# GLA heads in a lane of their own, a later first level, wider steps between mLSTM heads, and an urgent GpSimd multiplication

## The chip, the cores and the metric

One core of one Trainium2 chip runs the whole kernel; the other cores are idle. The metric is the device time of one launch in microseconds. Lower is better.

## What is computed

One inference step of a two-layer trunk, on 512 prompt tokens and 8 sequences of 4 sample tokens, 544 columns in all, in float32 throughout. The first layer's mixer is the place of the change:

```
mq, mk, mv, mo, mi, mf, gq, gk, gv, gg, ga = split(x @ w_in)        # 1024 -> 3096 columns
mLSTM, 4 heads, keys of 64, values of 128:   gates from mi, mf; scores (q k) * exp(decay);
    h = headnorm(num / max(|den|, exp(-m))) * sigmoid(mo)
GLA, 4 heads, keys of 64, values of 128:     la = log_sigmoid(ga @ wa2 + ba) / 16, cumulated to A
    s[t, s'] = sum_k q[t,k] k[s',k] exp(A[t,k] - A[s',k])  for s' <= t
    o = headnorm(s @ v + (q exp(A)) @ S0) * silu(gg)
both also return their last states, for the prompt and for every sample sequence
mix = concat(mLSTM, GLA) @ w_out;  x <- LN(1.414 x + mix);  then a squared-ReLU MLP
```

The second layer is a Mamba-2 mixer with an MLP of its own. The change leaves both, and the first MLP, as they are.

## The kernel before

**The dense work.** Activations lie with features on partitions and tokens in the free dimension, in two halves of 272 columns. A float32 product is made from three products of split operands (`whi`, `wlo` for a weight block, `xh`, `xl` for the activations). So one 128-column block of `w_in` is 2 halves x 8 k-tiles x 3 = 48 matmuls, all on line 378 in `dense`. The first stage, `ab`, has 24 such blocks in the order gq0 gk0 gq1 gk1, gv 0-3, mq, mk, mv 0-3, gg 0-3, mo 0-3. Before each matmul of line 378 stands one `tick()`.

**The lanes.** All other TensorE work of the stage is fed in between by generators. Each lane is a queue of generators; a generator emits some instructions, then yields a number n, and comes on again n + 1 ticks later. `need(keys)` yields 0 until the keys are set. TensorE executes in exactly the order in which this emits (its order is fixed by hand). The order on the other engines, VectorE, ScalarE, GpSimd and the DMA queues, is made by a planner ahead of time: it walks its own estimate of the execution and gives each engine the ready instruction of the highest priority, which is the order of emission, unless a block is marked `high_priority`. At run time every engine then takes its instructions strictly in that order. So an instruction whose input comes later than the planner thought holds all that stand behind it.

**The GLA lane.** `gla_decay` makes A for two feature groups q = 0, 1 (two heads each). `gla_scores` makes for each q the diagonal (`gd`, L1072, multiplied by the identity on L1074 into `sT`) and then nine levels L = 1, 2, 4 ... 256: GpSimd subtracts (`F`, L1083), ScalarE takes two exponentials (L1085, L1086), VectorE makes `zq` (L1090) and `zk` (L1092), TensorE multiplies them (`gs`, L1100 or L1113), and VectorE or ScalarE puts the result into `sT` (L1104, L1107 to L1114). `zq` and `zk` have two buffers each. A level comes 16 ticks after the one before. A transposition (`kdt`, L1122) ends each q. After both q, four heads follow. `head_out` of one head has two parts. The first multiplies the scores with the values (`num`, L868, two PSUM banks), and the headnorm is made from it: VectorE statistics (L872, L873), two ScalarE functions, and `hn` (L896), marked urgent. The second part transposes `hn` (`hot`, L902) and makes `cg` (L904). `pipeline` sets the second part of one head directly in front of the first part of the next, `W["out"]` = 38 apart. Then come the final state (`fst`), the GLA sample tokens and the mLSTM sample tokens, each with six state updates: GpSimd masks the values (`vm`, L1002), TensorE multiplies (`supd`, L1006), and VectorE adds into the state `c` (L1010), which goes out on SyncE's queue (`s_S` or `s_C`, L1015). The state of the mLSTM samples comes in on ScalarE's queue (L962) into the two buffers that held the GLA state.

**The mLSTM lane.** `ml_gates` has four parts of small ScalarE and VectorE work on four partitions (L1220 to L1275); part i waits until the first part of GLA head i has been emitted. The heads wait for the key `"gla"`, set when the last GLA head is done. Each has a broadcast (`rowbc`), scores (`md`, `mo`, L1318 to L1326) and the two parts of `head_out`; `pipeline` staggers them `W["mr"]` = 46 apart.

**Shared buffers.** `F`, `kd`, `hn`, `kz` and `vm` share four buffers (tag `sc`). Small PSUM tiles have four banks, every fifth of them another one.

**The start.** `warm` emits ten matmuls on constants; then the gate projections of the first half (`gate_sums(0)`, L842) come in two parts, 6 and 11 ticks later.

Of the kernel before, what the change touches and what calls it, by code (L numbers as in the profile page):

```python
# [13 lines left out]
ALU = mybir.AluOpType  # L14
# [3 lines left out]
P = 128  # L18
# [14 lines left out]
HEADM = 6  # L33
HEADA = 2

W = dict(dec=12, gates=30, gr=8, sc=16, lev=15, v=24, kd=10, out=38, ss=40, end=12, c0=20, u=13, s=16, ml=12, mr=46, dt=238, sg=72, sx=14, sq=26, so=48, l0=12, l1=12, v0=74, v1=55, f0=16, f1=18, f2=4, ls=20, vs=47)
GATES = ((0, 0, 4), (32, 4, 4), (64, 8, 16))
LEVELS = (64, 32, 16, 8, 4, 2, 1)

# [189 lines left out]
def trunk_kernel(ctx, tc, a, stages=("ab", "mlp0", "ssd", "mlp1")):  # L229
    nc = tc.nc  # L230
    V, S, G, TE = nc.vector, nc.scalar, nc.gpsimd, nc.tensor
# [99 lines left out]
    ready = set()  # L331

    def need(*keys):
        while not ready.issuperset(keys):
            yield 0

    def launch(gen, lane="norm"):
        lanes.setdefault(lane, []).append([next(gen), gen])
# [377 lines left out]
    def ab(pool, early, then):  # L716
# [120 lines left out]
        def gate_sums(hf):  # L837

            ps = pm("gsum")
            for k in range(KT):  # L840
                g = k % 4
                TE.matmul(ps[32 * g:32 * g + 32, :TH], gw[:, k], xs_in[4 * hf + k // 2][:, k % 2], start=k < 4, stop=k >= 4)  # L842
                if k == 3 and hf == 0:
                    yield 11
            with tc.high_priority():
                S.copy(gsum[hf], ps[:, :TH])

# [89 lines left out]
        def sample(key, q_, ksT, kstk, w, wl0, em):  # L937

            st_in, st_out = a["C0" if key == "m" else "S0"], a["s_C" if key == "m" else "s_S"]
            vs = vraw[key]
            nv = 129 if key == "m" else 128
            pbd = small("pbd", [P, NB, 4, LS])
            with hold():
                V.tensor_tensor(pbd, ksT.rearrange("p (b t) -> p b t", t=LS)[:, :, None, :].broadcast_to([P, NB, 4, LS]),
                                hmask[:, None, :, None].broadcast_to([P, NB, 4, LS]), ALU.mult)  # L950
                for q in range(2):
                    qw = small("qw", [P, NS])
                    V.tensor_tensor(qw, q_[q][:, NP:], w[:, q], ALU.mult)
                    for e in range(2):
                        o = 8 * q + 4 * e
                        V.tensor_tensor(Zq[:, q].rearrange("p (r x) -> p r x", r=2)[:, :, :128].rearrange("p r (k c) -> p r k c", k=4)[:, :, :, o:o + LS],
                                        qw.rearrange("p (k r t) -> p r k t", k=4, r=2),
                                        hm[:, e:e + 1, None, None].broadcast_to([P, 2, 4, LS]), ALU.mult)
            c0 = []
            for q in range(2):  # L960
                t = pool.tile([P, NB, 130], F32, tag="z4", name="c0", bufs=2)
                S.dma_start(out=t[:, :, :128], in_=st_in[:, q])  # L962
                if key == "m":
                    V.tensor_copy(t[:, :, 128:129], n0[:, q, :, None])
                c0.append(t)
            yield W["c0"]
            num = pm("snum")
            TE.matmul(num[:, :nv], pbd.rearrange("p b h t -> p (b h t)"), vs[:, :nv], start=True, stop=False)
            for r in range(2):
                for q in range(2):  # L970
                    for k in range(4):
                        TE.matmul(num[32 * k:32 * k + 32, :nv], Zq[:, q, 128 * r + 32 * k:128 * r + 32 * k + 32], c0[q][:, 2 * k + r, :nv],
                                  start=False, stop=r == 1 and q == 1)
            st, mv = small("sst6", [P, 6]), small("smv", [P, 2])
            with tc.high_priority():
                ns = small("sns", [P, 130], bufs=2)
                V.tensor_copy(ns[:, :nv], num[:, :nv])
                num = ns
                V.bn_stats(st, num[:, :128])
                V.bn_aggr(mv, st)  # L980
                f, nb, hn = small("sf", [P, 1]), small("snb", [P, 1]), ns[:, :128]
                if key == "m":

                    r = small("sr", [P, 1])
                    V.tensor_tensor(r, num[:, 128:129], em, ALU.max)
                    V.scalar_tensor_tensor(r, num[:, 128:129], -1.0, r, ALU.mult, ALU.max)
                    V.reciprocal(r, r)
                    V.tensor_tensor(f, r, r, ALU.mult)
                    V.tensor_tensor(f, f, mv[:, 1:2], ALU.mult)
                    S.activation(f, f, AF.Ln, bias=epsc)  # L990
                    S.activation(f, f, AF.Exp, scale=-0.5)
                    V.tensor_tensor(f, f, r, ALU.mult)
                else:
                    S.activation(f, mv[:, 1:2], AF.Ln, bias=epsc)
                    S.activation(f, f, AF.Exp, scale=-0.5)
                V.scalar_tensor_tensor(nb, mv[:, 0:1], -1.0, f, ALU.mult, ALU.mult)
                S.activation(hn, num[:, :128], AF.Identity, scale=f, bias=nb)
            for q in range(2):
                for b0, b1 in ((0, 3), (3, 6), (6, 8)):
                    nb = b1 - b0  # L1000
                    vm = sc("vm", [P, nb, 130])
                    G.tensor_tensor(vm, vs[:, None, :].broadcast_to([P, nb, 130]),  # L1002
                                    seqm[:, b0:b1, None].broadcast_to([P, nb, 130]), ALU.mult)
                    yield W["u"]
                    u = pm("supd")
                    TE.matmul(u[:, :130 * nb], kstk[:, q], vm.rearrange("p b c -> p (b c)"), start=True, stop=True)  # L1006
                    uv = u[:, :130 * nb].rearrange("p (b c) -> p b c", b=nb)
                    for b in range(b0, b1):
                        c = c0[q][:, b, :nv]
                        V.scalar_tensor_tensor(c, c, wl0[:, q, b:b + 1], uv[:, b - b0, :nv], ALU.mult, ALU.add)  # L1010
                if key == "m":
                    nn = small("nn", [P, NB])
                    V.tensor_copy(nn[:, :, None], c0[q][:, :, 128:129])
                    nc.sync.dma_start(out=a["s_n"][:, q], in_=nn)
                nc.sync.dma_start(out=st_out[:, q], in_=c0[q][:, :, :128])  # L1015
            yield W["s"]
            p = pm("sho")
            TE.transpose(p[:, :P], hn, ident)
            y = small("sy", [P, 4, NS], bufs=2)
            V.tensor_tensor(y.rearrange("p h (b t) -> p b h t", t=LS), p[:, :P].rearrange("p (b h t) -> p b h t", b=NB, h=4),  # L1020
                            gn[key][:, None, :, None].broadcast_to([P, NB, 4, LS]), ALU.mult)
            (gla if key == "g" else ml)["y"] = y


        gla = {}
# [19 lines left out]
        def gla_scores():  # L1045
# [14 lines left out]
            for q in range(2):  # L1060
# [4 lines left out]
                qm = pool.tile([P, 2, NP], F32, tag="z4", name="qm", bufs=2)  # L1065
                for e in range(2):
                    S.activation(qm[:, e], Q[q][:, :NP], AF.Identity, scale=hm[:, e:e + 1])
                yield W["sc"]
                for e in range(2):
                    p = pm("gd")  # L1070
                    for b in range(4):
# [51 lines left out]
                kt = pool.tile([P, 4, P], F32, tag="kdt", name="kdt", bufs=2)  # L1123
                S.copy(kt, p.rearrange("p (b c) -> p b c", b=4))
                gla["kst"].append(kt)

        def hold(what="last", mx=None):

# [242 lines left out]
        def gla_lane():  # L1371
            gla["cg"] = []
            yield from need(("gate", 0))
            yield W["dec"]
            yield from gla_decay()
            yield from gla_scores()
            launch(gla_sample_scores(), "ss")
            ready.add("gscores")
            yield from need("gvt")
            yield from pipeline([head_out(gla, "g", h, gla["sT"][h // 2][:, :, h % 2]) for h in range(4)], W["out"], (1, 0))  # L1380
            ready.add("gla")
            yield W["end"]
            final_state(gla["kst"], "g", a["p_S"])
            yield from need("sscores")
            yield from gla_samples()
            yield from need("mscores", "mvt")
            yield from ml_samples()

        def ml_lane():
            ml["cg"] = []  # L1390
# [10 lines left out]
        def warm():  # L1401

            w = pm("warm")
            for _ in range(10):
                TE.matmul(w[:, :P], ones, ones, start=True, stop=True)
            yield 6
            yield from gate_sums(0)

        launch(warm(), "warm")
        launch(gla_lane(), "gla")  # L1410
        launch(ml_lane(), "ml")
        lanes.setdefault("ss", [])
        heads = [ws.next() for _ in range(HEADA)]
# [706 lines left out]
```

## Time and profile before

| | |
|---|---|
| runs | 1500.14, 1498.67, 1499.76 us; median 1499.76 |
| profiled execution | 1500.9 us, its span 1499.2 us, mean granted TensorE clock 0.992 |
| TensorE matmul | 1470.2 us busy, 98% of the span |
| VectorE, ScalarE, GpSimd | 73%, 53%, 13% of the span |
| stage `ab` | the first 240 us or so of the span |

All times of the profile are microseconds from the first instruction, unless ns is said. "L378" is a line of the kernel. A row of the timeline gives the start, the duration, the engine, the line, the operation, what it writes and reads, how many, and in brackets how long the engine was idle ahead of it and what ended that. A row of the table by stretch gives the length, then busy time and number of instructions of TensorE (PE), its weight loads (PEld), VectorE (DVE), ScalarE (ACT) and GpSimd (POOL), then the granted clock (1.00 is full speed), the share of the DMA engines and GB/s.

### The profile page before, as it was taken

What the parts mean: (1) busy time and instruction counts of PE and PEld (TensorE: products, weight loads), DVE (VectorE), ACT (ScalarE), POOL (GpSimd) and SP (SyncE); (2) the same over time, 40 slices, a digit from 0 to 9 for tenths busy, and PEclk for the clock granted to TensorE, in tenths of its full rate; (3) what the DMA queues carried; (4) which work ended last, traced back from release to release, by engine and by line L of the source; (5) the groups of instructions that cost most, each with busy time, mean ns of one, the idle gap of its engine ahead of it and who ended that gap; (6) DMA issues with size and microseconds to landing.
All of it is one profiled execution on the core that took longest, in us unless ns stands there. A gap on an engine that the chain in (4) does not pass through costs nothing.

```text
span 1499.2 us, 29203 instructions
## 1 busy us (share of the span) xinstructions
PE 1470.2 (98%) x11607; PEld 1420.4 (95%) x11607; DVE 1094.2 (73%) x2075; ACT 795.2 (53%) x1750; POOL 190.1 (13%) x228
## 2 busy tenths in 40 slices
PE   9999989999999999999999999999999999999997
PEld 8999979999999999999888889989999999999996
DVE  6666576787677667668899987777678677676656
ACT  7544457474444434537786675555257354444343
POOL 2411132100000000010242441421010000000000
PEclk9999999999999999999999999999999999999999
DMA  7221332313233332416558766364222333233121
GB/s 245 65 71 43 89 131 83 128 49 103 72 112 99 91 93 85 154 52 201 131 146 255 237 191 224 99 210 146 71 75 68 98 99 98 86 99 95 61 85 60
DMA packets 95025, 172.51 MB, mean 115 GB/s; under 512 B 15880, under 2 KB 50968, under 8 KB 94632
## 3 DMA queue, kind: packets, MB, share of 16 engines
q1 hardware_dynamic: 62280, 140.44, 30.1%
q10 hardware_dynamic: 29216, 17.19, 4.4%
q0 software_dynamic: 3392, 13.00, 2.4%
q8 instruction: 91, 1.49, 0.4%
q14 instruction: 46, 0.38, 0.1%
HBM read 153.48 MB, written 17.13 MB: 114 GB/s over the span
## 4 chain that ended last, share of the span: by engine, by line
PE 42%; DVE 4%; DMA 3%; ACT 1%; issue 1%; POOL 0%; SPq 0%; ACTq 0%; DVEq 0%; POOLq 0%
PE psd L378 29%; PE psd L590 9%; DMA E<-d_cs 1%; PE yp L1698 1%; PE it L1745 1%; DVE acc L1592 1%; DVE wlo L168 1%; DMA ec<-d_ecs 1%; PE sp L1676 1%; PE sps L1752 1%; DMA wraw<-mlp_w 0%; DVE h0n L1758 0%; ACT E L1658 0%; PE xt L1637 0%; PE ip L1673 0%
## 5 line engine op out<-in xcount | busy, mean ns | idle before, releaser
L378 PE MATMUL psd<-xh,whi 128*128 128x272 f32 x1488 | 441.6, 297 | 0.5 <-ACT xh L287 0.5
L378 PE MATMUL psd<-xh,wlo 128*128 128x272 f32 x1488 | 435.9, 293 | 0.0
L378 PE MATMUL psd<-xl,whi 128*128 128x272 f32 x1488 | 434.3, 292 | 1.3 <-DVE xl L478 1.3
L378 PEld LDWEIGHTS psd<-xh,whi 128*128 128x128 f32 x1488 | 281.6, 189 | 8.8 <-issue 6.1
L378 PEld LDWEIGHTS psd<-xl,whi 128*128 128x128 f32 x1488 | 281.8, 190 | 7.4 <-issue 4.3
L378 PE MATMUL psd<-hh,whi 128*128 128x272 f32 x992 | 286.6, 289 | 0.0
L378 PE MATMUL psd<-hh,wlo 128*128 128x272 f32 x992 | 286.2, 288 | 0.0
L378 PE MATMUL psd<-hlo,whi 128*128 128x272 f32 x992 | 286.1, 288 | 0.0
L378 PEld LDWEIGHTS psd<-xh,wlo 128*128 128x128 f32 x1488 | 281.5, 189 | 3.9 <-issue 2.9
L167 ACT CAST whi<-wraw 128x1024 fp32r<-128x1024 f32 (+2 forms) x175 | 173.5, 997 | 147.3 <-PE psd L378 134.1
L168 DVE TENSOR_TENSOR wlo<-wraw,whi 128x1024 fp32r<-128x1024 f32 (+2 forms) x175 | 207.1, 1186 | 48.0 <-ACT whi L167 47.1
L378 PEld LDWEIGHTS psd<-hlo,whi 128*128 128x128 f32 x992 | 186.7, 188 | 0.2
L378 PEld LDWEIGHTS psd<-hh,whi 128*128 128x128 f32 x992 | 186.8, 188 | 0.2
L378 PEld LDWEIGHTS psd<-hh,wlo 128*128 128x128 f32 x992 | 186.7, 188 | 0.1
L428 DVE TENSOR_TENSOR xf<-xf,psd 128x272 f32<-128x272 f32 x208 | 88.1, 433 | 74.3 <-PE psd L378 73.8
L590 PE MATMUL psd<-xh,wlo 128*128 128x272 f32 x416 | 119.9, 288 | 0.0
L590 PE MATMUL psd<-xh,whi 128*128 128x272 f32 x416 | 119.8, 288 | 0.0
L590 PE MATMUL psd<-xl,whi 128*128 128x272 f32 x416 | 119.6, 288 | 0.0
L203 ACT CAST whi<-wsum 128x1024 fp32r<-128x1024 f32 x52 | 54.3, 1044 | 110.7 <-PE psd L590 70.2
L203 ACT CAST whi<-wraw 128x1024 fp32r<-128x1024 f32 (+1 forms) x52 | 43.4, 834 | 95.3 <-PE psd L378 84.2
L204 DVE TENSOR_TENSOR wlo<-wsum,whi 128x1024 fp32r<-128x1024 f32 x52 | 63.7, 1224 | 23.1 <-ACT whi L203 23.1
L590 PEld LDWEIGHTS psd<-xl,whi 128*128 128x128 f32 x416 | 78.4, 188 | 0.0
(488 smaller groups left out, 2827.8 us busy)
## 6 DMA issues: line engine op xcount, KB each, us to landing
wraw<-mlp_w SPq DMA_DIRECT2D x80, 512.0 KB, 3.7
wraw<-ssd_in SPq DMA_DIRECT2D x40, 512.0 KB, 4.1
wraw<-mlp_w SPq DMA_DIRECT2D x64, 256.0 KB, 3.0
wraw<-ab_in SPq DMA_DIRECT2D x22, 512.0 KB, 3.6
h<-h SPq DMA_DIRECT2D x32, 256.0 KB, 4.7
h0n<-h0n SPq DMA_DIRECT2D x16, 512.0 KB, 5.7
E<-d_cs ACTq DMA_DIRECT2D x16, 512.0 KB, 5.8
s_h<-h0n POOLq DMA_DIRECT2D x16, 512.0 KB, 3.9
```

What stands on the lines that cost most here:

```text
L167: nc.scalar.copy(hi[:, r], w[:, r])
L168: nc.vector.tensor_tensor(lo[:, r], w[:, r], hi[:, r].bitcast(F32), ALU.subtract)
L203: self.cut[0] = nc.scalar.copy(hi, x).ins
L204: self.cut[1] = nc.vector.tensor_tensor(lo, x, hi.bitcast(F32), ALU.subtract).ins
L378: last[0] = TE.matmul(ps[:, :TH], (hi, hi, lo)[t][:, k, :], (rh, rl, rh)[t], start=i == 0, stop=i == n - 1).ins
L428: V.tensor_tensor(x, x, ps, ALU.add)
L590: last[0] = TE.matmul(ps, wt[:, k], bt[:, k], start=first and n == 0, stop=n == 11, skip_group_check=not first).ins
L1592: V.scalar_tensor_tensor(acc[:, :n], ci[:, w:w + n], cw[:, m, w:w + 1], acc[:, :n], ALU.mult, ALU.add)
L1676: TE.matmul(sp, Bt[:, b], xw, start=True, stop=True)
L1698: TE.matmul(ypv[64 * e:64 * e + 64, j], z[:, 64 * r:64 * r + 64], E[:, r], start=True, stop=True)
L1745: TE.matmul(it[64 + NS * k:64 + NS * k + NS], Cm[:, NS * (q + k):NS * (q + k) + NS], h0[k], start=q == 0, stop=q == NB - 2)
L1752: TE.matmul(sp[:, 256 * j:256 * j + 256], Xs[:, m * P:(m + 1) * P], Bm.rearrange("p k n -> p (k n)"), start=True, stop=True)
```

## The change

- The constants: `out` 38 to 48, `mr` 46 to 52, new `hd` = 6 and `s0` = 50.
- The first feature group's diagonal, and with it all levels of that group, comes 51 instead of 17 ticks after the masked queries (`s0` in place of `sc` for q = 0).
- The GLA heads leave the GLA lane. `gla_heads` runs in a lane of its own: heads 0 and 1 wait for the first feature group alone, heads 2 and 3 for the second. Each head's second part comes 49 ticks after its first, and the next head's first part 7 ticks later. The old lane goes on with the levels of q = 1 and waits for `"gla"` ahead of the final state.
- The multiplication of `vm` (L1002) is marked urgent.
- The two yields of the gate projections become 12 and 5 instead of 6 and 11.

```diff
-W = dict(... out=38, ss=40, ... mr=46, ...)
+W = dict(... out=48, hd=6, s0=50, ss=40, ... mr=52, ...)
...
                 if k == 3 and hf == 0:
-                    yield 11
+                    yield 5
...
                     vm = sc("vm", [P, nb, 130])
-                    G.tensor_tensor(vm, vs[:, None, :].broadcast_to([P, nb, 130]),
-                                    seqm[:, b0:b1, None].broadcast_to([P, nb, 130]), ALU.mult)
+                    with tc.high_priority():
+                        G.tensor_tensor(vm, vs[:, None, :].broadcast_to([P, nb, 130]),
+                                        seqm[:, b0:b1, None].broadcast_to([P, nb, 130]), ALU.mult)
...
-                yield W["sc"]
+                yield W["sc"] if q else W["s0"]
...
                 gla["kst"].append(kt)
+                ready.add(("gT", q))
...
             ready.add("gscores")
-            yield from need("gvt")
-            yield from pipeline([head_out(gla, "g", h, gla["sT"][h // 2][:, :, h % 2]) for h in range(4)], W["out"], (1, 0))
-            ready.add("gla")
+            yield from need("gla")
             yield W["end"]
...
+        def gla_heads():
+            yield from need(("gT", 0))
+            for h in range(4):
+                yield from need(("gT", h // 2), ("gvt", h))
+                g = head_out(gla, "g", h, gla["sT"][h // 2][:, :, h % 2])
+                next(g)
+                yield W["out"]
+                next(g)
+                yield W["hd"]
+            ready.add("gla")
...
-            yield 6
+            yield 12
             yield from gate_sums(0)
 
         launch(warm(), "warm")
         launch(gla_lane(), "gla")
+        launch(gla_heads(), "gh")
         launch(ml_lane(), "ml")
```

More of the change, by code (lines that the diff above doesn't have):

```diff
@@ L34 @@
 HEADA = 2
-W = dict(dec=12, gates=30, gr=8, sc=16, lev=15, v=24, kd=10, out=38, ss=40, end=12, c0=20, u=13, s=16, ml=12, mr=46, dt=238, sg=72, sx=14, sq=26, so=48, l0=12, l1=12, v0=74, v1=55, f0=16, f1=18, f2=4, ls=20, vs=47)
+W = dict(dec=12, gates=30, gr=8, sc=16, lev=15, v=24, kd=10, out=48, hd=6, s0=50, ss=40, end=12, c0=20, u=13, s=16, ml=12, mr=52, dt=238, sg=72, sx=14, sq=26, so=48, l0=12, l1=12, v0=74, v1=55, f0=16, f1=18, f2=4, ls=20, vs=47)
 GATES = ((0, 0, 4), (32, 4, 4), (64, 8, 16))
```

## The prediction

> **What bounds the kernel.** I read first the page's head and its chain of waits, then the waits of TensorE, then busy time by stretch.
>
> ```profile
> span 1499.2 us, 29203 instructions
> ...
> PE 42%; DVE 4%; DMA 3%; ACT 1%; issue 1%; POOL 0%; SPq 0%; ACTq 0%; DVEq 0%; POOLq 0%
> ```
>
> The waits of TensorE in the first 240 us (in all, times, the longest), and four stretches:
>
> ```profile
> PE gs L1100 <- DVE zk L1092: 3.8, 1, 3.8
> PE supd L1006 <- POOL vm L1002: 3.1, 1, 3.1
> PE hot L902 <- ACT hn L896: 1.7, 2, 0.9
> PE warm L1405 <- DVE ones L281: 1.1, 1, 1.1
> PE psd L378 <- ACT xh L287: 0.5, 1, 0.5
> PE la L1035 <- ACT gate L853: 0.5, 1, 0.5
> PE gsum L842 <- DMA gw<-ab_gate: 0.3, 1, 0.3
> PE md L1318 <- ACT kz L1314: 0.3, 1, 0.3
> ```
>
> ```profile
> 40.00:102.00 62.00, 61.92 (x466) 59.96 (x466) 42.66 (x79) 29.11 (x69) 20.54 (x18) 0.95 0.23 68
> 140.00:160.00 20.00, 20.00 (x167) 19.06 (x169) 7.11 (x19) 7.50 (x17) 3.53 (x5) 0.91 0.21 64
> 193.00:226.00 33.00, 29.08 (x219) 25.83 (x220) 22.20 (x81) 16.55 (x42) 10.62 (x16) 0.95 0.33 117
> 330.00:360.00 30.00, 30.00 (x241) 30.00 (x241) 19.55 (x30) 13.32 (x24) 0.00 (x0) 1.00 0.37 106
> ```
>
> TensorE is the largest share of the chain, and the row of 330 to 360 shows it at its pace: 241 matmuls in 30 us, 0.1245 us for one, which is also the length of one tick. The change removes no matmul and adds none. What it can win is what `ab` loses: waits of TensorE (10.3 us in the eight rows, 9.2 without the first microsecond on the constants), and time at a lowered clock, length times one minus the granted clock (62 x 0.05 = 3.1 us, 20 x 0.09 = 1.8, 33 x 0.05 = 1.7). Together 15.8 us, and no gain of much more is to be had in this stage. What comes after it is not touched, and I take it as unmoved.
>
> **Where things go.** Counting ticks by the rule that a yield of n takes n + 1 gives the places in the dense stream, before and after. The diagonal of the first group stood at 152 and stands at 152 + 34 = 186; that group's transposition at 307 and 341; the second group's at 479 and 513. The first parts of the four GLA heads stood at 479, 518, 557, 596 (39 apart); they stand at 341, 397 (49 + 7 on), then, after the second group, 513 and 569. `"gla"` is set at 618 + 7 = 625 instead of 635 + 39 = 674. The mLSTM heads start there and go on by 53 instead of 47: their second parts at 815, 862, 909, 956 before, and 784, 837, 890, 943 after. GLA sample updates: 744 to 814 before, 696 to 766 after; mLSTM sample updates: 899 to 969, and 886 to 956. All is emitted before the last four blocks (tick 960 and on), so nothing of it runs bare at the end of the stage. Input weights come on SyncE's queue behind the sample stores, which move with the updates; five split buffers of some 6 us of dense work each stand between.
>
> **1. The first level later: -6.5 us.**
>
> ```profile
> 32.31 1.95 PE L1072 MATMUL gd<-qm,gk 128*128 128x128 f32 x16
> 37.18 1.26 DVE L1074 TENSOR_TENSOR sT<-gd,con 128x512 f32<-128x512 f32 x2
> 38.36 1.33 DVE L1090 TENSOR_TENSOR zq<-F,qm 128x512 f32<-128x512 f32 x1
> 39.61 0.41 DVE L1092 TENSOR_TENSOR zk<-gk,F 128x256 f32<-128x256 f32 x1
> 40.08 2.08 PE L1100 MATMUL gs<-zq,zk 128*128 128x128 f32 x8 [3.83 <-DVE zk L1092]
> 40.00:48.00 8.00, 7.92 (x43) 7.92 (x44) 5.20 (x8) 2.47 (x7) 3.49 (x3) 0.63 0.00 0
> ```
>
> The level came up at 40.08 - 3.83 = 36.25 and waited for `zk`, done at 40.02. The wait costs 3.83, and behind it the clock is 0.63 for 8 us: 8 x 0.37 = 3.0. Together 6.8. The new place is 34 x 0.1245 = 4.2 us later in dense work: the diagonal ends at 34.3 + 4.2 = 38.5, the level comes up at 40.5, half a microsecond behind `zk`. If VectorE still takes the diagonal (1.26) first, it starts that at 38.5 and `zk` is ready at 38.5 + 1.26 + 1.33 + 0.41 = 41.5: a wait of 1.0. Ends: -6.8, and -2.8 where the wait of 1.0 alone should lower the clock as much again. I take 0.3 of wait, since `zq` and `zk` don't need the diagonal, and so -6.5. The levels behind it come in clock time where they came before, since 6.8 us saved nearly make up for 34 ticks and their own work.
>
> **2. GLA heads beside the levels: -1.6, and +1.2 for the crowd.**
>
> ```profile
> 120.12 1.37 PE L902 MATMUL hot<-con,hn 128*128 128x128 f32 x4 [0.87 <-ACT hn L896]
> 128.90 0.60 PE L902 MATMUL hot<-con,hn 128*128 128x128 f32 x4
> L872 DVE BATCH_NORM_STATS2 bst<-num 128x6 f32<-128x128 f32 x12 | 2.9, 287 | 4.6 <-PE num L868 4.5
> L873 DVE BATCH_NORM_AGGREGATE bmv<-bst 128x2 f32<-128x6 f32 x12 | 1.8, 173 | 0.0
> L904 DVE TENSOR_SCALAR cg<-hot,prm 128x512 f32<-128x512 f32 x2 | 1.5, 748 | 2.8 <-PE hot L902 2.8
> L1227 DVE TENSOR_TENSOR_SCAN rw<-con,rw 4x544 f32<-4x544 f32 x1 | 1.3, 1282 | 0.0
> L1234 DVE TENSOR_TENSOR_SCAN rw<-rw 4x544 f32<-4x544 f32 x1 | 1.3, 1281 | 0.0
> L1226 DVE SCALAR_TENSOR_TENSOR rw<-rw 4x544 f32<-4x544 f32 x1 | 0.7, 715 | 0.0
> L1228 DVE TENSOR_TENSOR uw<-uw,rw 4x544 f32<-4x544 f32 x1 | 0.7, 714 | 0.0
> 68.00:84.00 16.00, 16.00 (x134) 15.87 (x133) 8.28 (x13) 6.63 (x16) 5.26 (x6) 1.00 0.22 67
> 79.85 0.41 DVE L1092 TENSOR_TENSOR zk<-gk,F 128x256 f32<-128x256 f32 x1
> 82.54 1.05 PE L1100 MATMUL gs<-zq,zk 128*128 128x128 f32 x8
> ```
>
> The wait of 0.87 and the stretching of the four transpositions (1.37 against 0.60) cost 1.64. With 49 ticks from first to second part in place of 39, and with levels in between, that second part comes over 1.2 us later. Ends -1.6 and 0; I take -1.6. In return heads 0 and 1 and the first two parts of the mLSTM gates now fall among the second group's levels. One head asks VectorE for 4 x 0.287 + 4 x 0.173 + 0.75 = 2.6 us, the first part of the gates for 1.28 + 1.28 + 0.72 + 0.71 = 4.0 and three small ones on top, 6.6 and more together, near the stretch of 68 to 84, where VectorE is busy 8.28 of 16 and has 7.7 to spare. It fits, barely; a level has `zk` done at 80.26 and comes up at 82.54, so 2.3 us of lateness are hidden. Ends 0 and +6.8 (one wait like that of part 1); I take 1.2, nearer the lower. This work leaves its old place, where the sample scores and the last heads get room.
>
> **3. The mLSTM heads, earlier and wider: -2.0.**
>
> ```profile
> 186.98 0.17 DVE L964 COPY c<-n 128x8 f32<-128x8 f32 x1 [2.67 <-DMA s_S<-c]
> 187.37 0.40 ACT L820 ACTIVATE gg<-psd 128x272 f32<-128x272 f32 x1 [5.49 <-DVE bst L872]
> 193.45 1.38 PE L902 MATMUL hot<-con,hn 128*128 128x128 f32 x4 [0.88 <-ACT hn L896]
> 196.00:200.00 4.00, 4.00 (x18) 3.21 (x17) 1.85 (x4) 0.00 (x0) 0.76 (x1) 0.57 0.00 0
> ```
>
> VectorE stood for 2.67 us and ScalarE for 5.49 behind the loading of the mLSTM sample state, whose buffer still held GLA state on its way out. The headnorm of mLSTM head 1 was behind both, so TensorE lost 0.88 + 0.78 (stretch) + 0.28 (`md`) and then 4 x 0.43 = 1.7 of clock: 3.7. After the change the last GLA update stands 784 - 766 = 18 ticks, 2.2 us, ahead of the first part of that head, in place of 1; the second part stands 53 ticks after, in place of 47, 0.7 us more. 2.9 us cover the 0.88. But the planner orders these queues anew, and the store may now hold up head 0 or the scores of head 2. Ends -3.7 and +1.5 (a wait as above with its stretch); I take -2.0.
>
> By the rule in the Trainium skill, page "TensorE: Matmul & The Clock Gate", section "Part 1", the clock halves after an idle window of about 3.4 us. The rows of part 1 agree with it (3.83 us of wait, then 0.63); the row of 196 to 200 doesn't, where the longest wait is 0.88. By the rule this part could win at most 1.9, and in proportion 1.0 in place of 2.0, and the sum would be 1490.3.
>
> **4. Urgent masked values: -1.6.**
>
> ```profile
> 216.95 0.69 POOL L916 TENSOR_TENSOR cg<-cg,gg 128x240 f32<-128x240 f32 x1 [2.84 <-DVE hf L892]
> 217.61 2.78 POOL L1002 TENSOR_TENSOR vm<-vstk,con 128x260 f32<-128x260 f32 x4
> ```
>
> Four multiplications stood on GpSimd behind one of `finish`, which waited 2.84 us for its gate; TensorE waited 3.1 for the first. Urgent, they go ahead of it, if the planner sees their buffers free by then; if it was the buffer that put them there, nothing moves. Ends -3.1 and 0; the middle, -1.6. What now waits behind them on GpSimd is `cg` of `finish` (0.7 us each), which nobody needs before the end of the stage, a dozen microseconds later. VectorE, which adds the updates, gets the same work in the same places.
>
> **5. The gate projections: 0.** Their first part moves behind six more matmuls; the second stays (6 + 11 = 12 + 5). The wait of 0.3 for the gate weights goes, but the next, 0.5, is for `xh`, which ScalarE sets; the stream can't pass it either way. Ends -0.8 and +0.5.
>
> **6. The lowered clock at 140 to 160: 0.** No wait stands there; the small gate products (four rows) come in the same clusters. Ends -1.8 and +1.8.
>
> **Sum:** -6.5 - 1.6 + 1.2 - 2.0 - 1.6 = -10.5 us. The profiled execution took 1500.9 (span 1499.2 and 1.7 around it), 1.1 above the median of the runs, 1499.76. On that median's scale: 1489.3 us. All lower ends together would be -6.8 - 1.6 - 3.7 - 3.1 - 0.8 - 1.8 = -17.8, 1482.
>
> **Rivals.**
> A. The crowd takes it back: VectorE's queue has gate scans ahead of `zq` and `zk`, one level of the second group (80 to 100 us) waits as long as the first does now, 6.8 with its clock, and the late parts win nothing. -6.5 - 1.6 + 6.8 = -1.3, or -4.9 with parts 3 and 4: 1495 to 1498.5. For it: 6.6 us and more into 7.7. Against it: 2.3 us of cover at a level, and the gates' chain alternates with ScalarE.
> B. The urgent values take the shared buffers from `F`.
>
> ```profile
> L1083 POOL TENSOR_TENSOR F<-A 128x512 f32<-128x512 f32 x14 | 16.9, 1211 | 22.3 <-DVE zk L1092 15.9 <-ACT whi L167 4.5 <-DVE zq L1090 2.0
> ```
>
> GpSimd's subtraction, 1.2 us, then can't run a level ahead; if half of it shows at each of nine levels, 5.4 us are lost: 1494.7. For it: `F` and `vm` share four buffers, and the GLA values are there long before their use. Against it: the edit marks the multiplication and not the buffer.
> C. Slower. The same place as A, but the lateness repeats: VectorE is over its time from head 0 to head 1 and again from head 1 on (the second part of the gates and its statistics), and three levels wait 6.8 each: +20.4 - 8.1 = +12, 1512. It decides from the second such wait: 13.6 against the 11.7 of all gains. For it: the tightest engine is VectorE in just this stretch. Against it: the first part of the gates is the only long one.
> D. It does nothing it says: the planner keeps the diagonal ahead and the values behind; -3, 1497.
>
> **How the numbers follow.** Forecast 0.6; A 0.18; B 0.07; C 0.08; D 0.07. Range 1484 to 1498.5: the lower end leaves out the case in which nearly all lower ends meet, the upper one takes in A, B and D and leaves out C. The forecast's own range, 1484 to 1494. About 0.2%, 3 us, is what can be told from no change here. Faster by more: the forecast, B, half of A and of D, with a little lost to places not named: 0.78. Within: the rest of A and D, and some of C's shallower forms: 0.13. Slower: 0.09.
>
> **What would show it.** Part 1: no wait of `gs` over 1.1 us before 48, granted clock 1.00 in 40 to 48. Part 2: `num` of two GLA heads at about 67 and 81 us, no wait of `gs` for `zk` from 76 to 104. Part 3: no `hot` wait past 160. Part 4: no `supd` wait for `vm`. Wrong it would be with a wait of `gs` in the second group, with `F` waiting for buffers, or with the clock below 1.00 in new places.

## The result, and the profile after

The changed kernel takes 1496.31 us (median of 18 runs, 1495.06 to 1499.84) against 1501.22 for the kernel before on the same chip (18 runs, 1497.69 to 1504.9): a ratio of 0.997, 95% interval 0.9962 to 0.9978, 4.9 us less. 10.5 us less had been forecast. The profiled execution took 1497.35 us, 3.6 less in its span than the one of before (1499.2), at a mean clock of 0.994 (before 0.992). So the direction was right and the size under half. Rival A, one level of the second group that waits, is what happened. That its end "-4.9 with parts 3 and 4" is also the measured difference is luck, since two of its terms were off in opposite directions (below).

Behind L1000 the lines of the changed kernel are one to twelve further down: its L1101 is L1100 before, its L1229 is L1227. First its head and the chain of waits, then the waits of TensorE in its first 245 us (in all, times, the longest), and five stretches:

```profile
span 1495.6 us, 29198 instructions
...
PE 42%; DVE 5%; DMA 2%; issue 1%; ACT 1%; POOL 0%; ACTq 0%; SPq 0%; DVEq 0%; POOLq 0%
```

```profile
PE gs L1101 <- DVE zk L1093: 9.0, 2, 7.4
PE warm L1416 <- DVE ones L281: 1.1, 1, 1.1
...
PE md L1320 <- ACT kz L1316: 0.2, 1, 0.2
```

```profile
40.00:48.00 8.00, 7.28 (x60) 7.06 (x59) 6.26 (x8) 3.68 (x9) 2.96 (x3) 1.00 0.02 5
140.00:160.00 20.00, 20.00 (x194) 18.66 (x193) 10.05 (x33) 8.42 (x21) 4.25 (x6) 1.00 0.20 61
193.00:226.00 33.00, 32.78 (x270) 30.76 (x269) 26.50 (x89) 18.47 (x46) 10.92 (x16) 1.00 0.42 137
96.00:100.00 4.00, 1.21 (x6) 1.24 (x7) 2.55 (x5) 3.35 (x8) 1.21 (x1) 0.50 0.00 0
100.00:104.00 4.00, 4.00 (x19) 4.00 (x19) 2.06 (x5) 2.53 (x6) 2.24 (x3) 0.50 0.00 0
```

The waits for `hn` and for `vm` are gone, and the clock is full in all three stretches where it had been below 1.00. What is left are two waits of `gs`, both in places where before has none; the row ahead of them is the first level:

```profile
41.33 1.05 PE L1101 MATMUL gs<-zq,zk 128*128 128x128 f32 x8
48.88 1.16 PE L1101 MATMUL gs<-zq,zk 128*128 128x128 f32 x8 [1.60 <-DVE zk L1093]
98.79 2.05 PE L1101 MATMUL gs<-zq,zk 128*128 128x128 f32 x8 [7.36 <-DVE zk L1093]
```

The first level comes up without a wait; the third waits 1.60. In the second group a level due at 98.79 - 7.36 = 91.43 gets its `zk` at 98.65. Behind the wait the clock is 0.50 up to 104 and 0.90 in the 4 us after: 1.2 x 0.5 + 4 x 0.5 + 4 x 0.1 = 3.0 us. What VectorE and then ScalarE did meanwhile:

```profile
83.53 2.01 DVE L168 TENSOR_TENSOR wlo<-wraw,whi 128x1024 fp32r<-128x1024 f32 x1 [0.20 <-DVE rw L1228]
85.57 2.05 DVE L1229 TENSOR_TENSOR_SCAN rw<-con,rw 4x544 f32<-4x544 f32 x1
...
90.73 0.49 DVE L872 BATCH_NORM_STATS2 bst<-num 128x6 f32<-128x128 f32 x2
92.35 1.28 DVE L1236 TENSOR_TENSOR_SCAN rw<-rw 4x544 f32<-4x544 f32 x1
97.11 0.69 DVE L1091 TENSOR_TENSOR zq<-F,qm 128x512 f32<-128x512 f32 x1 [1.03 <-ACT F L1086]
98.22 0.43 DVE L1093 TENSOR_TENSOR zk<-gk,F 128x256 f32<-128x256 f32 x1 [0.41 <-ACT F L1087]
```

```profile
82.65 0.38 ACT L828 COPY gv<-psd 128x272 f32<-128x272 f32 x1
92.35 0.30 ACT L878 ACTIVATE hf<-bmv,epsc 128x4 f32<-128x4 f32 x1 [9.33 <-DVE bmv L873]
94.46 1.51 ACT L896 ACTIVATE hn<-num,hb,hf 128x128 f32<-128x128 f32 x4 [0.81 <-DVE hb L893]
96.67 0.42 ACT L1086 ACTIVATE F<-F 128x256 f32<-128x256 f32 x1
```

It is a chain through two queues. On VectorE the weight split and the first gate scan stand ahead of the statistics of head 1, so these begin only at 90.73. On ScalarE that head's first function stands ahead of all else and idles 9.33 us for them; behind it stand the exponentials of the waiting level, which begin at 96.67, though GpSimd had made the level's differences by 88.5 (below). So VectorE was late once, ScalarE passed the lateness on to the level, and VectorE then waited for ScalarE.

### The profile page after: what moved, and what is told of

Read it like the earlier page. It is cut to its first block, busy times and chain, and to the rows that moved or that the text cites. A ratio compares the mean times of both kernels' runs of the same rounds, so it can differ in the third digit from the quotient of the medians.

```text
span 1495.6 us, 29198 instructions
## 1 busy us (share of the span) xinstructions
PE 1465.4 (98%) x11607; PEld 1416.8 (95%) x11607; DVE 1100.7 (74%) x2075; ACT 793.6 (53%) x1750; POOL 190.4 (13%) x228
## 4 chain that ended last, share of the span: by engine, by line
PE 42%; DVE 5%; DMA 2%; issue 1%; ACT 1%; POOL 0%; ACTq 0%; SPq 0%; DVEq 0%; POOLq 0%
PE psd L378 29%; PE psd L590 9%; DMA E<-d_cs 1%; PE yp L1710 1%; PE it L1757 1%; DVE wlo L168 1%; DVE acc L1604 1%; DMA ec<-d_ecs 1%; PE sp L1688 1%; PE sps L1764 1%; DVE h0n L1770 0%; PE ip L1685 0%; ACT E L1670 0%; DVE xf L552 0%; PE xt L1649 0%
```

## The experiments

All ratios are to the kernel before, run on the same chip beside each group (medians 1499.15, 1499.84 and 1499.33).

**1. Heads back in the GLA lane.** The rest of the change is kept.

```diff
-            yield from need("gla")
+            yield from need("gvt")
+            yield from pipeline([head_out(...) for h in range(4)], 38, (1, 0))
+            ready.add("gla")
...
-        launch(gla_heads(), "gh")
```

> The changed kernel with the four GLA heads back in the GLA lane behind both groups, 39 ticks apart; the later first level, the 53 ticks between mLSTM heads, the urgent values and the gate projections as changed. If the lane is what costs, no wait for zk over 1.7 us in 60 to 110 us, and 4 to 8 us faster than the changed kernel (0.991 to 0.995), with one hot wait of 1 to 2 us back near 120. Rival, the later first level itself shifts the levels into the wait: a wait of 4 us or more for zk in 80 to 105 stays, and the time is that of the changed kernel (0.997).

1492.69 us, 0.9959 [0.9945, 0.9973]. The only `gs` wait left is the third level's 1.6, so the lane is what made the wait of 7.4. The kernel is 1.7 us below the changed one by the ratios (3.6 by the medians), with intervals that overlap, and not 4 to 8 as expected: late waits come instead, 2.26 us for `hn` at 193 and 0.87 for `vm` at 218, which the lane does not have (experiment 5). The `hot` wait that was expected near 120 does not come back.

**2. Gates later.** The first part of the mLSTM gates also waits for the end of the second group's scores.

```diff
-            yield from need(("g", 0))
+            yield from need(("g", 0), "gscores")
```

> The changed kernel with one edit: the first part of the mLSTM gates waits until both groups' levels are over, not only for GLA head 0. The changed kernel waited 7.4 us for zk of the second group's level 8 (91.4 to 98.8 us), with a lowered clock behind it. Theory T1, the gates' five microseconds on VectorE hold up the statistics of head 1 and with them everything: the wait falls to 1.5 us or less, and the kernel gains 6 to 9 us on the changed one (ratio to before 0.991 to 0.993). Theory T2, the order on ScalarE alone, where the exponentials of level 8 stand behind the headnorm of head 1: that order is kept here, a wait of 3 us or more stays and the gain is 4 us or less (0.994 to 0.997).

1497.08 us, 0.9985 [0.9973, 0.9998]. The rows of its ScalarE and TensorE:

```profile
86.52 0.30 ACT L878 ACTIVATE hf<-bmv,epsc 128x4 f32<-128x4 f32 x1 [4.73 <-DVE bmv L873]
89.42 0.46 ACT L1086 ACTIVATE F<-F 128x256 f32<-128x256 f32 x1
```

```profile
91.09 1.13 PE L1101 MATMUL gs<-zq,zk 128*128 128x128 f32 x8 [0.89 <-DVE zk L1093]
131.76 1.11 PE L1279 MATMUL uwt<-con,uw 128*128 128x128 f32 x4 [5.23 <-ACT uw L1253]
```

```profile
102.00:140.00 38.00, 32.77 (x225) 30.85 (x223) 22.55 (x80) 18.08 (x45) 0.84 (x1) 0.87 0.19 56
```

ScalarE's queue still has the headnorm ahead of the exponentials, but its input comes at 86.5 instead of 92.3, and the level waits 0.89 instead of 7.36. So it was the gates on VectorE that made the wait long, as T1 said. The gain of T1 did not come: the gates are now late themselves, and 5.23 us for `uw` and a clock of 0.87 over 38 us eat it.

**3. Head 1 later.** It waits for the second group too; the gates stay.

```diff
-                yield from need(("gT", h // 2), ("gvt", h))
+                yield from need(("gT", min(1, (h + 1) // 2)), ("gvt", h))
```

> The changed kernel with one edit: GLA head 1 waits for the second group's transposition, as heads 2 and 3 do; head 0 and the first part of the gates stay among the levels. T2: the wait of 7.4 us for zk goes nearly entirely, since ScalarE reaches the exponentials ahead of any headnorm of head 1; 6 to 9 us faster than the changed kernel (0.991 to 0.993). T1: the gates still hold up VectorE, a wait of 2 to 4 us stays, in the same place (0.994 to 0.996).

1492.64 us, 0.9955 [0.994, 0.9971]. That is 2.2 us below the changed kernel by the ratios (3.7 by the medians), where T2 had 6 to 9. There are four small `gs` waits, 4.1 us together, none over 1.6. With the gates still among the levels but no headnorm of head 1 on ScalarE ahead of the exponentials, the long wait is gone as well: it takes both. The head's statistics leave VectorE together with its headnorm here, so this run does not tell the two apart; the rows of the changed kernel above do, in which the exponentials stand behind the headnorm.

**4. Both later.** Edits 2 and 3 together.

> The changed kernel with both cures: head 1 and the first part of the mLSTM gates held until the second group's scores are done. Theory (either cure alone takes the 7.4 away; the gates moved late cost a wait of 5.2 for uw at 131 us of their own): gs waits at most 2.5 us in all, of which 1.6 at the third level; the uw wait stays at 3 to 6 us; 0.998 to 0.9995 of before, worse than head 1 alone (0.9955). Rival (the uw wait came from head 1's headnorm on the same queues): it shrinks below 2 us, and 0.994 to 0.996.

1491.23 us, 0.9948 [0.9933, 0.9964]. My theory fell and the rival holds: no wait for `uw` any more, in its place 1.24 us for the sample scores. So what was late in experiment 2 needed that head's work on the same queues.

**5. The lane alone.** On the kernel before: the lane with `out=48, hd=6`, the first level where it was, `mr=46`, values not urgent.

```diff
-            yield from need("gvt")
-            yield from pipeline([head_out(...) for h in range(4)], W["out"], (1, 0))
-            ready.add("gla")
+            yield from need("gla")
...
+        launch(gla_heads(), "gh")
```

> The kernel before with part 2 alone: the GLA heads in a lane of their own (out=48, hd=6), the first level where it was, mr=46, values not urgent. Theory 1 (the lane puts VectorE's gate scans and ScalarE's headnorm functions among the second group's levels, and that is the whole loss of part 2): here too one level of the second group waits for zk, 4 to 8 us, near 85 to 100 us, with the clock lowered behind it, while the first level keeps its 3.8 and its lowered clock; the hot waits of 1.7 go. Time 1.002 to 1.006 of before. Rival (the lane only hurts together with the later first level, which moves the second group 34 ticks on and into the gates): no wait over 2 us at the second group, and 0.997 to 1.000 of before. Part 2 as predicted (-0.4 net) would be 0.9997.

1500.27 us, 1.0003 [0.9994, 1.0013]. The time is close to the rival's upper end, the trace is theory 1's:

```profile
39.72 1.16 PE L1100 MATMUL gs<-zq,zk 128*128 128x128 f32 x8 [3.83 <-DVE zk L1092]
97.35 2.08 PE L1100 MATMUL gs<-zq,zk 128*128 128x128 f32 x8 [7.35 <-DVE zk L1092]
```

```profile
90.16 0.30 ACT L878 ACTIVATE hf<-bmv,epsc 128x4 f32<-128x4 f32 x1 [7.15 <-DVE bmv L873]
```

```profile
193.00:226.00 33.00, 33.00 (x293) 31.08 (x293) 22.75 (x75) 19.17 (x50) 12.21 (x17) 1.00 0.39 133
```

The wait is 7.35 us with the first level early too, so it belongs to the lane and not to the 34 ticks. What the lane wins back is the late part: from 102 to 245 us TensorE waits for nothing, and the clock is 1.00, with `mr` at 46 and `vm` not urgent.

**6. The first level later, alone.** On the kernel before.

```diff
-                yield W["sc"]
+                yield W["sc"] if q else 50
```

> The kernel before with the later first level alone. Theory: the wait of 3.8 us and 3.0 us of lowered clock go, a wait of 1.6 for the third level comes, the late waits (hot at 193, supd at 218) stay: 5 us faster than before (0.9965). Rival, the late waits come from the same lateness and move or go too: 9 us or more (0.994).

1491.04 us, 0.9949 [0.9935, 0.9964]: better than the whole change, and close to what the rival said. The waits from 40 us on:

```profile
PE gs L1100 <- DVE zk L1092: 1.7, 1, 1.7
PE supd L1006 <- ACT vstk L804: 1.5, 1, 1.5
PE supd L1006 <- ACT hn L896: 1.1, 1, 1.1
PE hot L902 <- ACT hn L896: 0.6, 1, 0.6
PE md L1318 <- ACT kz L1314: 0.5, 1, 0.5
```

```profile
193.00:226.00 33.00, 31.70 (x258) 29.55 (x259) 24.21 (x86) 16.44 (x43) 11.28 (x17) 1.00 0.41 134
```

The wait of 3.1 for `vm`, the wait of 0.9 at 120 us, and the lowered clock are gone with no edit to the late work.

**7. Urgent values alone.** On the kernel before.

```diff
+                    with tc.high_priority():
                         G.tensor_tensor(vm, ...)
```

> The kernel before with part 4 alone: the masked values urgent. As predicted, the supd wait for vm of 3.1 us near 217 shrinks to between 0 and 1.5 and the time falls by 1.6, 0.999 of before. Rival, from the run of the first level alone (in which that wait went with no edit to vm at all): the wait moves to another producer of the same chain (the values, or the store), and the time is 0.999 to 1.001; the early wait of 3.8 stays in both.

1499.6 us, 1.0 [0.9988, 1.0011]. The mark moves no instruction: the two programs are the same, so this run is a second execution of the kernel before. Its rows and stretches, to be read against those of before:

```profile
213.24 0.69 POOL L916 TENSOR_TENSOR cg<-cg,gg 128x240 f32<-128x240 f32 x1 [2.83 <-DVE hf L892]
213.90 2.78 POOL L1003 TENSOR_TENSOR vm<-vstk,con 128x260 f32<-128x260 f32 x4
```

```profile
40.00:48.00 8.00, 7.18 (x47) 7.19 (x48) 6.34 (x9) 3.51 (x9) 3.50 (x3) 0.79 0.00 0
140.00:160.00 20.00, 20.00 (x196) 19.02 (x197) 8.31 (x28) 8.47 (x19) 3.53 (x5) 1.00 0.24 75
196.00:200.00 4.00, 4.00 (x36) 4.00 (x36) 3.04 (x16) 2.00 (x4) 0.00 (x0) 1.00 0.02 4
```

The same multiplications stand behind the same `cg`, and TensorE waits the same 3.13 us (its row stands in the last section). In the changed kernel too, the program without the mark is the same, instruction for instruction.

**8. Wider steps alone**, and **9. the changed kernel without them.**

```diff
-W = dict(... mr=46, ...)
+W = dict(... mr=52, ...)
```

> The kernel before with part 3's constant alone: mr 52 in place of 46. As predicted, the hot wait of 0.88 at 193 and the clock of 0.57 behind it go: 0.998 to 0.999 of before. Rival, from the run of the first level alone (in which the lowered clock at 193 to 226 went with mr at 46): the wait there comes from the mLSTM sample state and its store, not from the distance between heads, and stays or moves: 0.9995 to 1.001. In both the first level's 3.8 stays.

> The changed kernel with mr back at 46. Part 3 as predicted (6 ticks more between the heads cover a late headnorm): a hot wait of 0.5 to 1.5 us comes back near 190, with a lowered clock behind it, and the time is 1 to 3 us above the changed kernel's, 0.998 to 0.9995 of before. Rival (the waits there went with the reordered lanes, as they did with the first level alone and with the lane alone, both at 46): no such wait, the 7.4 of the second group stays, and 0.996 to 0.998, the changed kernel's own time within 1 us.

Alone: 1498.18 us, 0.9991 [0.9979, 1.0002]. The `hot` wait at 193 turns into one of another TensorE instruction, a transposition for the mLSTM samples (`mkt`), 2.13 us for `hn`, and the clock over 193 to 226 stays at 0.95:

```profile
194.14 0.33 PE L1364 MATMUL mkt<-con,gkz 128*128 128x128 f32 x1 [2.13 <-ACT hn L896]
```

The changed kernel with 46: 1497.12 us, 0.9981 [0.9971, 0.9992], beside 1496.31 and 0.997 [0.9962, 0.9978] for the changed kernel, with intervals that overlap; no `hot` wait comes back, one of 1.19 at 172 for another `hn` does, and the 7.36 stays. In neither place is the constant worth anything that can be told. It may even cost: a wait of 1.8 to 2.3 us for `hn` at this `mkt`, between 189 and 194 us, stands in five of the seven kernels with 52 (here, in experiments 1, 3 and 4, and in experiment 3 with `s0=62`), and in no kernel with 46.

**10 to 12. Other places for the first level.** On the kernel before with 62 and with 56 in place of 50, and experiment 3 with `s0=62`.

```diff
-                yield W["sc"]
+                yield W["sc"] if q else 56
```

> The kernel before with the first group's diagonal 63 ticks after its masked queries (51 in the change). With 51 alone the third level still waits 1.7 us for zk at 48 us, since zq stands on VectorE behind a weight split and the first level's masked copy. If that lateness is fixed in time, 12 ticks more (1.5 us) cover it: no gs wait over 0.4 before 60 us, 0.9935 to 0.9945 of before, 1.0 to 1.5 us below the run with 51. If the wait hangs on the masked copy, which waits for the first level and moves with it, the wait stays at 1 to 2 us and the time at 0.9945 to 0.9955; a wait in the second group or later, which now comes nearer to the heads, would bring it to 0.996 or above.

> The changed kernel with head 1 held until the second group's scores are done and the first group's diagonal at 62 in place of 50. With head 1 held alone the level waits were 4.1 us in four (1.6 of it at the third level) and the time 0.9955. Theory (the third level's wait is a fixed lateness that 12 ticks cover, as they did in the kernel before with 62 alone; the late waits are small because the heads stand in a lane): the 1.6 goes, 1 to 3 us of gs waits remain in the second group, no wait of supd over 1 us, 0.994 to 0.995 of before. Rival (the 12 ticks push the second group's levels and the sample updates together again, as the kernel before with 62 alone showed with 6.6 us of supd waits): a new wait of 3 us or more between 80 and 226 us, 0.996 to 0.998.

> The kernel before with the first group's diagonal at 56. At 50 the third level waits 1.7 us and the late waits are 1.5 + 1.1 + 0.6; at 62 the third level waits nothing and vm comes late by 3.4 and 3.2. If the late waits grow with the place, this lies between: a gs wait of 0.6 to 1.2, supd waits of 1 to 4, 0.995 to 0.997. If they are set by the order that the planner happens to choose, either end is possible: no supd wait over 1 us and 0.993 to 0.9945, or 3 us and more and 0.997 to 0.999.

With 62: 1496.17 us, 0.9982 [0.9971, 0.9993]. No `gs` wait at all, as expected, but two late ones for `vm`, 3.44 and 3.12 us. The first:

```profile
175.02 0.69 POOL L916 TENSOR_TENSOR cg<-cg,gg 128x240 f32<-128x240 f32 x1 [8.53 <-DVE hb L893]
175.67 1.63 POOL L1002 TENSOR_TENSOR vm<-vstk,con 128x390 f32<-128x390 f32 x2
```

```profile
176.56 1.67 PE L1006 MATMUL supd<-vm,gkstk 128*128 128x390 f32 x2 [3.44 <-POOL vm L1002]
```

Here the planner put `vm` behind a `cg` that idles 8.53 us for its gate. Experiment 3 with 62 has the same fault once: 1494.47 us, 0.9968 [0.9956, 0.998], the rival's, with 3.35 us at 215.58 for a `vm` that stands behind a `cg`. With 56: 1486.39 us (5 runs, 1485.79 to 1487.41), 0.9913 [0.9898, 0.9929], 13 us below before and the fastest kernel here. Its span is 1484.1. Its rows:

```profile
166.37 0.84 POOL L1002 TENSOR_TENSOR vm<-vstk,con 128x390 f32<-128x390 f32 x1 [0.49 <-PE mo L1325]
```

```profile
190.08 0.66 PE L902 MATMUL hot<-con,hn 128*128 128x128 f32 x4 [0.97 <-ACT hn L896]
```

```profile
40.00:102.00 62.00, 62.00 (x488) 59.79 (x487) 43.82 (x80) 30.27 (x73) 18.63 (x18) 1.00 0.25 77
193.00:226.00 33.00, 33.00 (x279) 31.45 (x278) 26.01 (x90) 18.32 (x49) 11.22 (x17) 1.00 0.38 133
```

TensorE is busy from 40 to 102 without a gap, `vm` stands ahead of its `cg`, and the one wait past 40 us over 0.2 is 0.97. The late waits do not grow with the place (2.6 us for state updates at 50, 0.2 at 56, 6.6 at 62): they follow the order that the planner falls into. Why it takes one order or the other stays open.

## Why the prediction was right and wrong

**The step that failed is the "+1.2 for the crowd" of part 2.** It measured 7.36 us of wait and 3.0 of clock, 10.4. The count of VectorE had 6.6 us and more, for one head and the first part of the gates together, into 7.7 of spare time. In the changed kernel that part of the gates alone takes 5.7 us of VectorE (82.61 to 93.63), the second part follows it, and from 80.4 to 96.1 VectorE is never idle for more than 0.20 us. Two things were wrong besides. I took the cover of a level (2.3 us) as if each level met the load alone, and did not follow ScalarE's queue, where a headnorm that waits for VectorE stands ahead of a level's exponentials. Experiments 2, 3 and 5 show that the lane, the gates and head 1 meet there. And the durations came from quiet places: the scan (1.28 us in before) took 2.05 and the split (1.25 on the mean of its shape in before) 2.01, while GpSimd ran the level's differences. The split in before, all of this shape together, and GpSimd in the changed kernel:

```profile
L168 DVE TENSOR_TENSOR wlo<-wraw,whi 128x1024 fp32r<-128x1024 f32 x151 | 188.6, 1251 | 41.2 <-ACT whi L167 40.5
```

```profile
83.36 5.12 POOL L1084 TENSOR_TENSOR F<-A 128x512 f32<-128x512 f32 x3
```

By the Trainium skill, page "SBUF — State Buffer", section "Who interferes with whom", a VectorE instruction with two SBUF inputs contends with a GpSimd instruction that reads SBUF, and the port pair that they share is an exclusive lock. The rows agree: three of GpSimd's differences, 1.21 us each on the mean of before, took 5.12 beside the split and the scan. In experiment 3 the same scan took 2.03 and the split 2.06, and the long wait did not come, so the overlap alone does not make it. No run takes the overlap away by itself, so how much of the 7.36 it made is open.

**Part 1** won 3.83 + 3.0 and lost 1.60 at the third level: -5.2, where -6.5 was said. The 1.0 that I feared at the first level did not come; I had not looked at the third, whose `zq` stands behind a weight split and a masked copy. 56 covers it.

**Part 2's gain**, -1.6, came whole: no `hot` row in the changed kernel waits. But it was not the lane's own: with the first level alone at 50 (experiment 6) or at 56 the `hot` wait at 120 is gone too, and at 62 it is back (0.77 and 0.30).

**Parts 3 and 4** won all of 3.7 and 3.1 in the trace where -2.0 and -1.6 were said, but not by the edits they were booked on: the urgent mark is inert (experiment 7), and `mr` alone trades one wait for another (8, 9). The late waits went because the lane, or the later first level, each alone, changed the planner's order (5, 6). Bounding by the wait was right, naming its cause from one row of one queue was not.

**Parts 5 and 6.** The gate projections gave nothing that can be told. The dip at 140 to 160, 1.8 us, was no term of the program: experiment 7, the same program as before, has 1.00 there, and 0.79 instead of 0.63 behind the same 3.8 us wait.

By the traces: -5.2 - 1.6 + 10.4 - 3.7 - 3.1 - 1.8 = -5.0, beside 3.6 in the spans and 4.9 in the medians; the 1.4 us between the sum and the spans were not traced to a place. The upper bound of the prediction was added up wrongly: its eight rows of waits make 11.3 us and not 10.3 (10.2 without the first), so that the stage loses 16.8 us and not 15.8. That no change gains much more than this held: the run with 56 has a span 15.1 us shorter (13 in the medians; the span of before varies with its clock, as the last section shows).

Of the rivals, A is shown, with its place (one level of the second group, 91 us); its price was 6.8 and is 10.4, and the late parts won 6.8 where its end had 3.6 for them, so that the two errors nearly cancel in its -4.9. C, the same lateness at three levels, did not occur: one level waits long. B did not occur, since the mark does nothing. Of D, only that the values stay behind is true.

## What to carry to other kernels

A lane of work that "fits" into an engine's spare time must be followed through every in-order queue that it enters: ask what stands behind its waiting instructions, here a level's exponentials behind a headnorm's. Before booking a wait's removal on an edit, see whether the edit changes the order of that queue at all. And where a planner orders the queues, sweep the one constant that decides (here one place, 50, 56, 62) before restructuring: the better value won more than twice what the whole change did.

## What was not expected of the hardware

The clock behind a wait is not fixed by its length. The run with urgent values alone is the program of before, with the same waits; these are its rows at two of them, and the stretches around the second:

```profile
191.42 1.38 PE L902 MATMUL hot<-con,hn 128*128 128x128 f32 x4 [0.80 <-ACT hn L896]
214.56 1.12 PE L1007 MATMUL supd<-vm,gkstk 128*128 128x260 f32 x2 [3.13 <-POOL vm L1003]
```

```profile
211.31:214.72 3.41, 0.28 (x2) 0.16 (x2) 2.14 (x7) 1.56 (x6) 1.48 (x3) 1.00 1.02 416
214.72:218.13 3.41, 3.41 (x14) 3.21 (x15) 0.95 (x3) 1.14 (x4) 1.96 (x3) 0.50 0.89 337
```

Behind the wait of 0.80 its clock stayed 1.00 (196 to 200, shown above), where before had 0.57 behind 0.88; behind 3.13 it fell to 0.50 for 3.41 us, where before kept 1.00. These are a low stretch of before, and the two stretches that its wait of 3.13 lies across (it ended at 218.28):

```profile
196.06:199.47 3.41, 3.41 (x12) 2.62 (x12) 1.78 (x3) 0.00 (x0) 0.74 (x1) 0.50 0.00 0
213.13:216.54 3.41, 2.01 (x15) 1.69 (x13) 2.72 (x9) 2.42 (x7) 0.98 (x2) 1.00 0.92 318
216.54:219.95 3.41, 1.67 (x11) 1.62 (x12) 1.92 (x7) 1.50 (x4) 3.00 (x5) 1.00 1.02 415
```

Cut where it changes, the clock in this stage of the two executions is either 1.00 or 0.50, and it is 0.50 for 3.41 us or for twice that. In before the low stretches start at 39.05, 141.45 and 196.06 us, which is 102.40 and 54.61 apart, 30 and 16 times 3.413. So the clock changes on a grid of 3.413 us, and the grid lies differently in each execution. In before one of its edges, 196.06 + 6 x 3.413 = 216.54, cuts the wait of 3.13: TensorE is busy for 2.01 us of the window ahead of that edge and for 1.67 of the one behind, and the clock stays. In the other execution the wait lies whole within 211.31 to 214.72, TensorE is busy for 0.28 us of that window, and the next is at 0.50.

Executions of one program thus differ (the spans are 1499.2 and 1496.4), so a term taken from the granted clock of one execution is uncertain by some 3 us here. By the Trainium skill, page "TensorE: Matmul & The Clock Gate", section "Part 1", activity is judged in free-running windows of 3.4 us, so the same gap may fall in one window or across two. The rows of the wait of 3.13 agree with that. The lowered clock behind 0.88, which the prediction held against the rule, is no feature of the program. How much work within a window keeps the clock up is not shown: before has the lower clock also behind a window in which TensorE is busy for 2.27 of 3.41 us (192.65 to 196.06), and behind one in which it is busy throughout (138.04 to 141.45).
